# The FFN's output projection as a 2x2 block product of seven block products

## The chip, the core and the metric

The kernel runs on one core of a Trainium2 chip. The metric is device time in microseconds (us) of one execution. The engines are named as in the profile: PE is TensorE (matrix products, with PEld its weight loads), DVE is VectorE, ACT is ScalarE, POOL is GpSimd, SP is SyncE, which issues the DMAs.

## The reference

Two layers (DEPTH = 2) over a sequence of 512 rows of width 1024, in float32. Each layer is a token mixer (retention, chunk attention, differential attention, gates, a merge and one output projection), a layer norm, a SwiGLU FFN with 2816 hidden columns, and a second layer norm:

```python
x = _layer_norm(DEEPNORM_ALPHA * x + mix, ln1_g[l], ln1_b[l])
u = jnp.einsum('bsd,df->bsf', x, w_ffn_in[l])
u_gate, u_up = jnp.split(u, 2, axis=-1)
ffn = jnp.einsum('bsf,fd->bsd', jax.nn.silu(u_gate) * u_up, w_ffn_out[l])
x = _layer_norm(DEEPNORM_ALPHA * x + ffn, ln2_g[l], ln2_b[l])
```

The second einsum, 512 x 2816 by 2816 x 1024, is the output projection that is changed.

## The kernel before

Tiles have 128 rows. The sequence is NT = 4 row tiles `t`, the width KT = 8 tiles or two halves `hf` of 512 columns, the hidden width FT = 22 tiles. A float32 operand is carried as a pair `hi`, `lo` of float32r (class `Pair`; `split` makes it: ACT writes `hi`, DVE writes `lo`), and every product of two tiles is three matmuls (`mm3`): hi·hi, hi·lo, lo·hi. A weight (`Wt`) is loaded by SP into a staging tile `st` of up to 128 x 2048, cast by ACT to `wh` (L131) and subtracted by DVE to `wl` (L132), in two parts of 128 x 1024. There are NSTAGE staging tiles, AHEAD pairs of `wh` and `wl`, 8 PSUM banks and NSLOT = 60 slots of 128 x 512 in SBUF for everything else.

The program is a list of items, each with its weights and a function that issues its work. `run_items` takes the items in order and fetches weights of later items until AHEAD of them are ready. A list scheduler of the framework then sets the order of the instructions on each engine, from the order in which they were issued and from what they wait for; on each engine they run strictly in that order.

In the FFN a unit `u_ffn(i)` makes hidden tile i: 24 matmuls 512 wide for the gate, 24 for the other half, into two banks `pt`; ACT and DVE (`ffn_done`) turn them into `fth` and split it into the pair `hid[i]`. The first item, `u_ffn_first(2)`, does two units in halves of the sequence, since the transposes of the later half of the layer norm's rows come in its middle. Behind all 22 units comes the output projection, with hidden tiles as the stationary operand: `u_fout(hf, kb)` takes four hidden tiles and one weight 512 x 512 into four banks `pf`, one for each row tile; first all of half 0, then half 1, whose last four weights are one item, `u_fout_last`. That is 22 x 4 x 2 x 3 = 528 matmuls a layer. In this last item each row tile is finished on its own: residual and statistics (`fout_done`), and for the last layer `finish` (normalise and scale, store to the output), for the first layer `normalise` and, one row tile later, `transposes`, which put the rows into columns `xT` for the next layer (PE into banks `px`, ACT and DVE into pairs `xTh`, `xTl`). `natural` scales the rows and saves them.

The next layer begins with `u_first`: retention's first queries and keys (RQ, RK, 256 columns each) and the two halves of the values' weights; it starts on the first half of the sequence (256 columns) and calls `transposes(2)` and `transposes(3)` (`hooks`) behind that.

Of the kernel before, what the change touches and what calls it, by code (L numbers as in the profile page):

```python
# [2 lines left out]

# [8 lines left out]
F32 = mybir.dt.float32  # L12
# [28 lines left out]
PACKW = [512, 512, 256]  # L41

NSLOT = 60
AHEAD = 4
NSTAGE = 2
NLAST = 4


@with_exitstack
def trunk(ctx, tc, x_in, w_in, ret_norm_g, da_norm_g, lq1, lk1, lq2, lk2, w_a, w_b, w_c, b_merge, w_out,  # L50
# [23 lines left out]
    def bank(name="ps"):  # L74
        return psp.tile([P, 512], F32, tag="ps", name=name)
# [30 lines left out]
    class Wt:  # L106


        def __init__(self, pieces, nk, meanwhile=None):
# [19 lines left out]
            for a in range(0, nk, h):  # L129
# [3 lines left out]
                if meanwhile is not None and a == 0:  # L133
                    meanwhile()

    def proj_T(act, wt, c0, nk=KT, ps=None, half=None):
# [9 lines left out]
    def proj_T_half0(act, jobs, hook=None):  # L146

        for k in range(KT):
            a = act[k]
            if k == KT // 2 and hook is not None:  # L150
                hook()
# [102 lines left out]
    class Norm:  # L254
# [40 lines left out]
            if j == 1:  # L295
                self.to_T(hf)

        def to_T(self, hf):
            cols = slice(256 * hf, 256 * hf + 256)
            for k in range(KT):  # L300
# [32 lines left out]
    def run_items():  # L333
        ready, at = [], 0

        def fetch():
            nonlocal at
            specs, at = items[at][0], at + 1
            ready.append([])
            for sp in specs:  # L340
                first = at == 1 and not ready[-1]
                if first:
                    load_x(0, 2)
                ready[-1].append(Wt(*sp, meanwhile=first_x if first else None))
# [20 lines left out]
        load_x(2, NT)  # L365

    xTs = [[None] * KT for _ in range(DEPTH + 1)]
    hooks = {0: [lambda: start["n"].transposes(2), lambda: start["n"].transposes(3)]}

    def layer(l):  # L370
        lambda_init = 0.8 - 0.6 * math.exp(-0.3 * l)
# [78 lines left out]

        def u_first():

            def fn(wq, wk, *wv):
                ret_tables()
                pq, pk = [None] * 2, [None] * 2
                for j in range(2):
                    pq[j], pk[j] = bank("pt"), bank("pt")
                jobs = [(w, P * j, p[j]) for w, p in ((wq, pq), (wk, pk)) for j in range(2)]
                for js in ((jobs[:2], jobs[2:]) if l == 0 else (jobs,)):
                    proj_T_half0(xT, js)  # L460
                for hook in hooks[l]:
                    hook()
                for t in range(2):
                    rv_part(0, wv, t)
                for w, p, dst in ((wq, pq, rq), (wk, pk, rk)):
                    for j in range(2):
                        rqk_done(dst, j, proj_T(xT, w, P * j, ps=p[j], half=1))
                for t in range(2, NT):
                    rv_part(0, wv, t)
                vectors()  # L470
            return [([wcols(RQ, 256)], KT), ([wcols(RK, 256)], KT)] + rows_of(W, RV), fn

        def u_rg(hp):
            def fn(*wts):
# [304 lines left out]
            return mid, [s_d0(h, j)]  # L779

        for (specs, fn), *groups in [
            (u_first(),), (u_rg(0), [], [], [s_r1(0)], []),
            (u_rqk(rq, RQ, 1), [], [s_r2(0)]), (u_rqk(rk, RK, 1), [s_r1(1)], [s_r3(0)]),
            (u_rv(1), [s_r2(1)], [], [s_r3(1)], [s_r1(2)]), (u_rg(1), [], [s_r1(3)], [], []),
            (u_vhl(cv, CV, 64), [s_r2(2)], [s_r2(3)], [s_r3(2)], [s_r3(3)]), (u_cqk(0),),
            (u_gate(0, 0), *c(0)), (u_branch(0, 0), *c(1)), (u_cqk(1),),
# [63 lines left out]
        def ffn_spec(i):  # L850
            w = w_ffn_in[l]
            return ([w[:, P * i:P * i + P], w[:, FFN + P * i:FFN + P * i + P]], KT)

        def ffn_done(i, pg, pu):
# [7 lines left out]
        def u_ffn_first(n):  # L862
            def fn(*wts):
                pg, pu = [bank("pt") for _ in range(n)], [bank("pt") for _ in range(n)]
                proj_T_half0(x1T, [(wts[i], P * j, p[i]) for i in range(n) for j, p in enumerate((pg, pu))],
                             lambda: x1["n"].transposes(3))
                for i in range(n):
                    proj_T(x1T, wts[i], 0, ps=pg[i], half=1)
                    proj_T(x1T, wts[i], P, ps=pu[i], half=1)
                    ffn_done(i, pg[i], pu[i])  # L870
                for t in range(2, NT):
                    x1["n"].natural(t)
            return [ffn_spec(i) for i in range(n)], fn

        def u_ffn(i):
            def fn(wt):
# [2 lines left out]
                ffn_done(i, pg, pu)  # L879
            return [ffn_spec(i)], fn  # L880

        item(*u_ffn_first(2))
        for i in range(2, FT):
            item(*u_ffn(i))

        last = l == DEPTH - 1
        fo = {}
        x2 = {}

        def fout_done(hf, t):  # L890
            residual(x1["z"][t][hf], fo[hf][t])
            x2["n"].stats(t, hf)

        def u_fout(hf, kb):

            spec = rows_of(w_ffn_out[l], 512 * hf, 0, FT)[kb]

            def fn(wt):
                if kb == 0:
                    fo[hf] = [bank("pf") for _ in range(NT)]  # L900
                    if hf == 0:
                        load_res(saved[2 * l])
                        x2["n"] = Norm(x1["z"], v["g2"], v["b2"], bcast_rows(ln2_g[l:l + 1]),
                                       bcast_rows(ln2_b[l:l + 1]), xTs[l + 1], out if last else saved[2 * l + 1])
                for t in range(NT):
                    proj_N(hid, [wt], t, fo[hf][t], 4 * kb, kb == 0, 4 * kb + wt.nk == FT)
                    if 4 * kb + wt.nk == FT:
                        fout_done(hf, t)
            return [spec], fn

        def u_fout_last(kb):

            def fn(*wts):
                n = x2["n"]
                for t in range(NT):
                    proj_N(hid, wts, t, fo[1][t], 4 * kb, False, True)
                    if t in (1, 2) and not last:
                        n.transposes(t - 1)
                    fout_done(1, t)
                    if last:  # L920
                        n.finish(t)
                    else:
                        n.normalise(t)
                if not last:
                    n.natural(0)
                    n.natural(1)
            return rows_of(w_ffn_out[l], 512, 0, FT)[kb:], fn

        nb = -(-FT // 4)
        for kb in range(nb):  # L930
            item(*u_fout(0, kb))
        for kb in range(nb - NLAST):
            item(*u_fout(1, kb))
        item(*u_fout_last(nb - NLAST))

        def hook(t):
            def fn():
                x2["n"].transposes(t)
                if t == 3:
                    x2["n"].natural(2)  # L940
                    x2["n"].natural(3)
            return fn

        hooks[l + 1] = [hook(2), hook(3)]

    for l in range(DEPTH):
        layer(l)
# [47 lines left out]
```

## Time and profile before

| | |
|---|---|
| median of 3 runs | 1973.05 us (1972.7 to 1973.13) |
| the profiled execution | 1973.74 us, its span 1972.0 us |
| PE busy | 1953.1 us, 99% |
| DVE busy | 1045.0 us, 53% |
| ACT busy | 788.6 us, 40% |
| DMA | 203.21 MB, mean 103 GB/s |
| granted PE clock, mean | 0.998 |

The span is the stretch from the first to the last recorded event of the execution. Busy times of one engine are added up from single instructions; since matmuls are pipelined, the recorded duration of one is longer than the distance from its start to the next one's start. In the lines of a timeline stand the start, the duration, the engine, the line of the kernel, the operation, output<-inputs and, in brackets, the engine's idle time before and what ended it. In the lists of groups the numbers are the sum of busy time, the mean of one in ns and the idle time before.

### The profile page before, as it was taken

To read this page: it belongs to the slowest core of one execution; us is meant where nothing else is said; L and a number is where in the kernel's file an instruction comes from. 1 tells how busy PE (TensorE), PEld (TensorE's weight loads), DVE (VectorE), ACT (ScalarE), POOL (GpSimd) and SP (SyncE) were. 2 spreads that over 40 slices of the span, in tenths; PEclk is the share of its full clock that TensorE was granted. 3 is DMA by queue.
4 is the path that set the end of the run, shared out by engine and by line. 5 is a ranking of instruction groups with operands and counts; after the bars stand their busy time and mean duration, and the time that the engine had idled before them with its cause. 6 is when DMAs were issued, how large, how long until landed. Compare 5 with 4: busy or idle time off the path is not lost.

```text
span 1972.0 us, 23963 instructions
## 1 busy us (share of the span) xinstructions
PE 1953.1 (99%) x9506; PEld 1647.8 (84%) x9506; DVE 1045.0 (53%) x1918; ACT 788.6 (40%) x1431; POOL 48.2 (2%) x73
## 2 busy tenths in 40 slices
PE   8999999999999999999999999999999999999998
PEld 7888888888888888888898888888888898888886
DVE  4664556577557434333375545655774684343333
ACT  4443445466534322221154434555674343232220
POOL 0000000000000000000000000000000000000000
PEclk9999999999999999999999999999999999999999
DMA  5421332232145333242143223232221633332421
GB/s 187 135 89 56 118 102 82 74 97 75 64 150 163 106 96 100 92 159 97 62 163 118 75 86 102 76 90 86 86 86 48 209 109 111 102 95 98 160 75 43
DMA packets 222197, 203.21 MB, mean 103 GB/s; under 512 B 6926, under 2 KB 179076, under 8 KB 222084
## 3 DMA queue, kind: packets, MB, share of 16 engines
q1 hardware_dynamic: 222084, 201.67, 32.3%
q8 instruction: 75, 1.23, 0.3%
q14 instruction: 38, 0.31, 0.0%
HBM read 193.26 MB, written 8.39 MB: 102 GB/s over the span
## 4 chain that ended last, share of the span: by engine, by line
PE 98%; DVE 1%; DMA 0%; issue 0%; ACT 0%; SPq 0%; POOL 0%; DVEq 0%; ACTq 0%
PE pt L102 20%; PE pt L104 20%; PE pt L103 20%; PE pn L102 5%; PE pn L104 5%; PE pn L103 5%; PE pf L104 4%; PE pf L102 4%; PE pf L103 4%; PE ptr L238 1%; PE pco L625 1%; PE psc L209 1%; PE psc L208 1%; PE pdo L698 1%; PE po L104 1%; PE po L103 1%
## 5 line engine op out<-in xcount | busy, mean ns | idle before, releaser
L102 PE MATMUL pt<-xTh,wh 128*128 128x512 f32 (+1 forms) x1600 | 599.1, 375 | 4.6 <-ACT xTh L86 3.5
L103 PE MATMUL pt<-xTl,wh 128*128 128x512 f32 (+1 forms) x1600 | 596.0, 373 | 0.2 <-DVE xTl L92 0.2
L104 PE MATMUL pt<-xTh,wl 128*128 128x512 f32 (+1 forms) x1600 | 595.7, 373 | 0.0
L132 DVE TENSOR_TENSOR wl<-st,wh 128x1024 fp32r<-128x1024 f32 (+1 forms) x346 | 391.3, 1152 | 269.2 <-ACT wh L131 264.1
L131 ACT CAST wh<-st 128x1024 fp32r<-128x1024 f32 (+1 forms) x346 | 334.7, 997 | 483.5 <-PE pt L103 279.5
L102 PEld LDWEIGHTS pt<-xTh,wh 128*128 128x128 f32 x1600 | 302.2, 189 | 56.6 <-ACT xTh L86 3.9
L104 PEld LDWEIGHTS pt<-xTh,wl 128*128 128x128 f32 x1600 | 301.9, 189 | 53.1
L103 PEld LDWEIGHTS pt<-xTl,wh 128*128 128x128 f32 x1600 | 302.4, 189 | 51.8 <-DVE xTl L92 0.5
L102 PE MATMUL pn<-wh,xTh 128*128 128x512 f32 x384 | 151.0, 393 | 0.5 <-ACT lnt L307 0.5
L103 PE MATMUL pn<-wl,xTh 128*128 128x512 f32 x384 | 149.6, 390 | 0.0
L104 PE MATMUL pn<-wh,xTl 128*128 128x512 f32 x384 | 149.6, 390 | 0.0
L102 PE MATMUL pf<-wh,hidh 128*128 128x512 f32 x352 | 137.1, 390 | 0.0
L104 PE MATMUL pf<-wh,hidl 128*128 128x512 f32 x352 | 137.0, 389 | 0.0
L103 PE MATMUL pf<-wl,hidh 128*128 128x512 f32 x352 | 136.9, 389 | 0.0
L858 DVE TENSOR_TENSOR fth<-fth,pt 128x512 f32<-128x512 f32 x44 | 30.2, 687 | 170.3 <-PE pt L104 170.3
L104 PEld LDWEIGHTS pn<-wh,xTl 128*128 128x128 f32 x384 | 72.1, 188 | 15.2
L102 PEld LDWEIGHTS pn<-wh,xTh 128*128 128x128 f32 x384 | 72.1, 188 | 14.8 <-ACT lnt L307 0.7
L103 PEld LDWEIGHTS pn<-wl,xTh 128*128 128x128 f32 x384 | 72.2, 188 | 14.0
L857 DVE SCALAR_TENSOR_TENSOR fth<-fth,pt 128x512 f32<-128x512 f32 x44 | 30.2, 687 | 91.5 <-ACT fth L856 91.5
L103 PEld LDWEIGHTS pf<-wl,hidh 128*128 128x128 f32 x352 | 66.1, 188 | 13.7
L104 PEld LDWEIGHTS pf<-wh,hidl 128*128 128x128 f32 x352 | 66.1, 188 | 13.7
L102 PEld LDWEIGHTS pf<-wh,hidh 128*128 128x128 f32 x352 | 66.1, 188 | 13.6
(180 smaller groups left out, 2421.5 us busy)
## 6 DMA issues: line engine op xcount, KB each, us to landing
st<-in_w_in SPq DMA_DIRECT2D x55, 1024.0 KB
st<-in_w_ffn_in SPq DMA_DIRECT2D x88, 512.0 KB
st<-in_w_ffn_out SPq DMA_DIRECT2D x20, 1024.0 KB
st<-in_w_in SPq DMA_DIRECT2D x32, 512.0 KB
st<-in_w_branch_a SPq DMA_DIRECT2D x8, 1024.0 KB
st<-in_w_out SPq DMA_DIRECT2D x8, 1024.0 KB
saved<-z SPq DMA_DIRECT2D x24, 256.0 KB
z<-saved SPq DMA_DIRECT2D x24, 256.0 KB
```

The lines of the kernel that those rows point to most:

```text
L102: nc.tensor.matmul(ps, lh, rh, start=start, stop=False)
L103: nc.tensor.matmul(ps, lh, rl, start=False, stop=False)
L104: nc.tensor.matmul(ps, ll, rh, start=False, stop=stop)
L131: nc.scalar.copy(self.hi[:, a:b], st[:, a:b])
L132: nc.vector.tensor_sub(self.lo[:, a:b], st[:, a:b], f(self.hi[:, a:b]))
L208: nc.tensor.matmul(ps[:, :w], self.q[j][:, n], self.k[j][:, :w], start=True, stop=False)
L209: nc.tensor.matmul(ps[:, :w], self.q[j][:, n], self.kl[j][:, :w], start=False, stop=True)
L238: nc.tensor.transpose(ps[:, o + P * (nt - mt):o + P * (nt - mt) + P], E[pk][:, c + P * mt:c + P * mt + P], ident)
L625: nc.tensor.matmul(*x, start=mt == 0 and x is hi, stop=mt == NT - 1 and x is hi)
L698: nc.tensor.matmul(ps[:, 256 * j:256 * j + 256], pT[b].hi[:, o:o + P], vt[:, c:c + 256], start=mt == 0, stop=False)
L857: nc.vector.scalar_tensor_tensor(t, t, 1.0, pg, op0=ALU.add, op1=ALU.mult)
L858: nc.vector.tensor_mul(t, t, pu)
```

## The change

The output projection is done as a 2x2 block product with seven block products instead of eight. The hidden tiles are taken in three groups (`GROUPS`): first tile 0 with 2 x 4 tiles, 8 with 2 x 4, 16 with 2 x 3. Within a group the 512 rows are two halves, the group's hidden tiles two halves of kh tiles, the 1024 output columns two halves. `Quarters` takes two hidden tiles (i and i + kh) and makes the sums of row halves and tiles (`sa`, `sb`) and splits them: pairs `q11`, `q2`, `s12`, `s43`. `Halves` loads blocks of the weight and adds or subtracts them on DVE (`t1` to `t4`; `sa` is a staging tile of its own), `Staged` splits the result. Each product `m1, y, x, m2, v, g, h` runs for two row tiles j with kh x 3 matmuls, so that a layer has 7 x 2 x 22/2 x 3 = 462. Its bank is added to the residual `z` on DVE (`plus`), in `x` by way of `w` and `wy`, two copies that ACT made.

The items of a group's products are put between the units of the next group: a product, then one `u_ffn`. The last group has none behind it; its `g` and `h` are one item with two weights, which takes the place of `u_fout_last` (statistics, `finish` or `normalise`, `transposes`). AHEAD goes from 4 to 3, NSTAGE from 2 to 3. `u_first` now has three query and key weights (RQ, RK, RQ + 256), all three by halves of the sequence, with the transposes of the later rows in four parts (`transposes_of`) inside the third; the values' weights become an item of their own, and one item of the mixer's list goes.

```diff
-AHEAD = 4
-NSTAGE = 2
-NLAST = 4
+AHEAD = 3
+NSTAGE = 3
+GROUPS = [(0, 4), (8, 4), (16, 3)]
...
+    class Halves:
...
+        def t1(self):
+            self.add(self.a, self.load(0, 1))
+            return self.block(self.a)
...
+        def t4(self):
+            b, a = self.load(1, 0), self.__dict__.pop("a")
+            for s in self.parts():
+                nc.vector.scalar_tensor_tensor(b[:, s], a[:, s], -1.0, b[:, s], op0=ALU.mult, op1=ALU.subtract)
+            return self.block(b)
...
+    class Quarters:
...
+            nc.vector.tensor_sub(sa[:, a], t1[:, b], t2[:, b])
+            nc.vector.tensor_sub(sa[:, b], t1[:, a], sa[:, a])
+            nc.vector.tensor_sub(sb[:, a], t2[:, a], sa[:, b])
+            nc.vector.tensor_sub(sb[:, b], t1[:, b], t1[:, a])
+            q, p2, p12, p43 = g(F32R, "q11"), Pair("q2"), Pair("s12"), Pair("s43")
...
         def u_first():
-            def fn(wq, wk, *wv):
+            def fn(*wts):
...
+                banks.append([bank("pt") for _ in range(2)])
+                proj_T_half0(xT, [(wts[2], P * j, banks[2][j]) for j in range(2)],
+                             {2 * b: functools.partial(hooks[l], b) for b in range(4)})
...
         def ffn_done(i, pg, pu):
...
-            hid[i] = Pair("hid")
-            split(hid[i], t, scale=0.5)
+            hid[i] = t
+            r0, kh = next(x for x in GROUPS if x[0] <= i < x[0] + 2 * x[1])
+            if i >= r0 + kh:
+                hid[i - kh] = Quarters(hid[i - kh], hid[i], scale=0.5)
+                hid[i] = None
...
+        def plus(t, hf, ps, op, final=False):
...
+                nc.vector.tensor_tensor(z, z, ps, op=op)
+            if final:
+                x2["n"].stats(t, hf)
...
+            def x(wt):
+                for j in range(2):
+                    ps = run("x", j, wt)
+                    u = w.pop(j)
+                    nc.vector.tensor_sub(u, ps, u)
+                    plus(2 + j, 0, u, ALU.subtract)
+                    nc.vector.tensor_add(u, u, w.pop(("y", j)))
+                    plus(2 + j, 1, u, ALU.add)
+                    plus(j, 1, u, ALU.add)
...
+            def vv(wt):
+                for j in range(2):
+                    plus(j, 1, run("v", j, wt), ALU.add, end)
+                    if end:
+                        (x2["n"].finish if last else x2["n"].normalise)(j)
+
+            def g_(j, wt):
+                ps = run("g", j, wt)
+                plus(2 + j, 1, ps, ALU.add, end)
+                plus(2 + j, 0, ps, ALU.subtract)
+
+            def h_(j, wt):
+                ps = run("h", j, wt)
+                if end and not last:
+                    x2["n"].transposes(j)
+                plus(2 + j, 0, ps, ALU.subtract, end)
+                if end:
+                    (x2["n"].finish if last else x2["n"].normalise)(2 + j)
...
+            its = [([hv.b11], m1), ([hv.t1], y), ([hv.t2], x), ([hv.b21], m2), ([hv.b22], vv)]
+            return its + ([([hv.t3, hv.t4], gh)] if end else [([hv.t3], gg), ([hv.t4], hh)])
...
+        for gi in range(len(GROUPS)):
+            ids = tiles(gi + 1) if gi + 1 < len(GROUPS) else []
+            for it in fout_items(gi):
+                item(*it)
+                if ids:
+                    item(*u_ffn(ids.pop(0)))
```

How the instructions move, at three places. In the order's rows stand the line, the operation, output<-inputs, the shape and, for equal neighbours, their count.

DVE where layer 0 ends, before: `z` are the rows of the residual, `pf` a bank of the output projection, `bn`, `mv`, `rs` the norm's statistics, `bc` its scale, `xTl` the columns for the next layer.

```order
L285 TENSOR_SCALAR z<-z,mv,rs 128x512 x2
L805 SCALAR_TENSOR_TENSOR z<-z,pf 128x512
L314 TENSOR_TENSOR z<-z,bc 128x512
L92 TENSOR_TENSOR xTl<-lnt,xTh 128x256
L263 BN_STATS bn<-z 128x6
L315 TENSOR_TENSOR z<-z,bc 128x512
L92 TENSOR_TENSOR xTl<-lnt,xTh 128x256
```

And the same place in the changed kernel (`wl<-st,wh` of L134 are weights of the next layer's `u_first`):

```order
L997 TENSOR_TENSOR z<-z,pf 128x512
L419 TENSOR_TENSOR z<-z,bc 128x512
L997 TENSOR_TENSOR z<-z,pf 128x512 x2
L134 TENSOR_TENSOR wl<-st,wh 128x1024 x4
L357 BN_STATS bn<-z 128x6 x2
L374 BN_AGGR mv<-bn 128x2
L997 TENSOR_TENSOR z<-z,pf 128x512
L376 TENSOR_SCALAR rs<-mv 128x1
L94 TENSOR_TENSOR xTl<-lnt,xTh 128x256
L379 TENSOR_SCALAR z<-z,mv,rs 128x512 x2
```

The first `xTl` now stands behind additions to `z` of all products and behind four splits of the next unit's weights.

PE at the same place, before: the transposes of a row tile (`px`), followed by more products of the output projection.

```order
L104 MATMUL pf<-wh,hidl 128x512
L294 MATMUL px<-ident,z 128x128 x8
L102 MATMUL pf<-wh,hidh 128x512
L103 MATMUL pf<-wl,hidh 128x512
L104 MATMUL pf<-wh,hidl 128x512
```

And in the changed kernel, around the second set of transposes:

```order
L104 MATMUL pf<-wh,q2h 128x512
L105 MATMUL pf<-wl,q2h 128x512
L106 MATMUL pf<-wh,q2l 128x512
L388 MATMUL px<-ident,z 128x128 x8
L104 MATMUL pt<-xTh,wh 128x256 x3
L105 MATMUL pt<-xTl,wh 128x256
```

Directly behind the second transposes now stands the next layer's first unit; the first transposes have two products of nine matmuls behind them.

DVE at the end of the program, before:

```order
L275 SCALAR_TENSOR_TENSOR z<-z,rs,bc 128x512 x2
L805 SCALAR_TENSOR_TENSOR z<-z,pf 128x512
L263 BN_STATS bn<-z 128x6
L268 BN_AGGR mv<-bn 128x2
L270 TENSOR_SCALAR rs<-mv 128x1
L273 SCALAR_TENSOR_TENSOR z<-z,mv,bc 128x512 x2
L275 SCALAR_TENSOR_TENSOR z<-z,rs,bc 128x512 x2
```

And changed:

```order
L193 SCALAR_TENSOR_TENSOR st<-sa,st 128x512 x3
L206 TENSOR_TENSOR wl<-st,wh 128x512 x3
L997 TENSOR_TENSOR z<-z,pf 128x512 x2
L357 BN_STATS bn<-z 128x6 x2
L997 TENSOR_TENSOR z<-z,pf 128x512 x2
L357 BN_STATS bn<-z 128x6 x2
L362 BN_AGGR mv<-bn 128x2
L997 TENSOR_TENSOR z<-z,pf 128x512
L364 TENSOR_SCALAR rs<-mv 128x1
L367 SCALAR_TENSOR_TENSOR z<-z,mv,bc 128x512 x2
L369 SCALAR_TENSOR_TENSOR z<-z,rs,bc 128x512 x2
```

Before, one row tile's half was left for the end; now weight sums and splits, the additions of the last four products and all four row tiles' finishing follow one another in DVE's queue.

More of the change, by code (lines that the diff above doesn't have):

```diff
@@ L1 @@
+import functools
 import math
@@ new lines, in trunk, with __init__ @@
+    class Quarters:
+        def __init__(self, t1, t2, scale=None):
+            a, b = slice(0, 256), slice(256, 512)
+            sa, sb = g(name="sa"), g(name="sb")
+            nc.vector.tensor_sub(sa[:, a], t1[:, b], t2[:, b])
[3 more added lines that the diff above has]
+            q, p2, p12, p43 = g(F32R, "q11"), Pair("q2"), Pair("s12"), Pair("s43")
+            part_hi(q[:, a], t1[:, a], scale)
+            part_lo(q[:, b], t1[:, a], q[:, a], scale)
+            split(p2, t2, scale=scale)
+            split(p12, sa, scale=scale)
+            split(p43, sb, scale=scale)
+            self.use = {"m1": (q[:, a], q[:, b])}
+            for names, pr in ((("m2", "h"), p2), (("y", "x"), p12), (("v", "g"), p43)):
+                for name, sl in zip(names, (a, b)):
+                    self.use[name] = (pr.hi[:, sl], pr.lo[:, sl])
@@ L144, in proj_T, with proj_T_half0 @@
         return ps
-    def proj_T_half0(act, jobs, hook=None):
+    def proj_T_half0(act, jobs, hooks):
         for k in range(KT):
             a = act[k]
-            if k == KT // 2 and hook is not None:
-                hook()
+            if k in hooks:
+                hooks[k]()
             for wt, c0, ps in jobs:
@@ L296, in transposes, with transposes_of, to_T @@
                 self.to_T(hf)
-        def to_T(self, hf):
+        def transposes_of(self, hf, b):
+            ps = bank("px")
+            self.banks[hf] = {b: ps}
+            for k in (2 * b, 2 * b + 1):
+                for j in range(2):
+                    o = 256 * (k % 2) + P * j
+                    nc.tensor.transpose(ps[:, o:o + P],
+                                        self.z[2 * hf + j][k // 4][:, P * (k % 4):P * (k % 4) + P], ident)
+            self.to_T(hf, (2 * b, 2 * b + 1))
+        def to_T(self, hf, ks=range(KT)):
             cols = slice(256 * hf, 256 * hf + 256)
-            for k in range(KT):
+            for k in ks:
                 if self.xT[k] is None:
@@ L367, in trunk @@
     xTs = [[None] * KT for _ in range(DEPTH + 1)]
-    hooks = {0: [lambda: start["n"].transposes(2), lambda: start["n"].transposes(3)]}
+    hooks = {0: lambda b: start["n"].transposes_of(1, b)}
     def layer(l):
@@ L911, in u_fout_last @@
[L911 to L944, printed above, removed]
+        def plus(t, hf, ps, op, final=False):
+            z = x1["z"][t][hf]
+            if (t, hf) in x2["fresh"]:
+                x2["fresh"].remove((t, hf))
+                nc.vector.scalar_tensor_tensor(z, z, ALPHA, ps, op0=ALU.mult, op1=op)
+            else:
+                nc.vector.tensor_tensor(z, z, ps, op=op)
+            if final:
+                x2["n"].stats(t, hf)
@@ new lines, in fout_items, with run, m1, y @@
+        def fout_items(gi):
+            r0, kh = GROUPS[gi]
+            end = gi == len(GROUPS) - 1
+            hv = Halves(w_ffn_out[l], r0, kh)
+            w = {}
+            def run(name, j, wt):
+                ps = bank("pf")
+                for k in range(kh):
+                    hi, lo = hid[r0 + k].use[name]
+                    sl = slice(P * j, P * j + P)
+                    mm3(ps, hi[:, sl], lo[:, sl], wt.hi[:, k], wt.lo[:, k], k == 0, k == kh - 1)
+                return ps
+            def m1(wt):
+                if gi == 0:
+                    load_res(saved[2 * l])
+                    x2["fresh"] = {(t, hf) for t in range(NT) for hf in range(2)}
+                if end:
+                    x2["n"] = Norm(x1["z"], v["g2"], v["b2"], bcast_rows(ln2_g[l:l + 1]),
+                                   bcast_rows(ln2_b[l:l + 1]), xTs[l + 1], out if last else saved[2 * l + 1])
+                for j in range(2):
+                    ps = run("m1", j, wt)
+                    w[j] = g(name="w")
+                    nc.scalar.copy(w[j], ps)
+                    plus(j, 0, ps, ALU.add)
+            def y(wt):
+                for j in range(2):
+                    ps = run("y", j, wt)
+                    w["y", j] = g(name="wy")
+                    nc.scalar.copy(w["y", j], ps)
+            def x(wt):
+                for j in range(2):
+                    ps = run("x", j, wt)
[5 more added lines that the diff above has]
+                    plus(j, 1, u, ALU.add)
+            def m2(wt):
+                for j in range(2):
+                    plus(j, 0, run("m2", j, wt), ALU.add, end)
+            def vv(wt):
+                for j in range(2):
+                    plus(j, 1, run("v", j, wt), ALU.add, end)
[10 more added lines that the diff above has]
+                plus(2 + j, 0, ps, ALU.subtract, end)
+                if end:
+                    (x2["n"].finish if last else x2["n"].normalise)(2 + j)
+            def gg(wt):
+                for j in range(2):
+                    g_(j, wt)
+            def hh(wt):
+                for j in range(2):
+                    h_(j, wt)
+            def gh(wg, wh):
+                for j in range(2):
+                    g_(j, wg)
+                    h_(j, wh)
+                if not last:
+                    x2["n"].natural(0)
+                    x2["n"].natural(1)
+            its = [([hv.b11], m1), ([hv.t1], y), ([hv.t2], x), ([hv.b21], m2), ([hv.b22], vv)]
+            return its + ([([hv.t3, hv.t4], gh)] if end else [([hv.t3], gg), ([hv.t4], hh)])
@@ new lines, in tiles @@
+        def tiles(gi):
+            r0, kh = GROUPS[gi]
+            return [r0 + i + kh * j for i in range(kh) for j in range(2)]
+        ids = tiles(0)
+        item(*u_ffn_first(ids[:2]))
+        for i in ids[2:]:
+            item(*u_ffn(i))
+        for gi in range(len(GROUPS)):
[4 more added lines that the diff above has]
+                    item(*u_ffn(ids.pop(0)))
+            for i in ids:
+                item(*u_ffn(i))
```

108 lines of the change are left out of this document (64 added, 44 removed).

## The prediction

> **What bounds the kernel now.** I read the page first: busy shares, chain of waits, costliest groups.
>
> ```profile
> span 1972.0 us, 23963 instructions
> PE 1953.1 (99%) x9506; PEld 1647.8 (84%) x9506; DVE 1045.0 (53%) x1918; ACT 788.6 (40%) x1431; POOL 48.2 (2%) x73
> PE 98%; DVE 1%; DMA 0%; issue 0%; ACT 0%; SPq 0%; POOL 0%; DVEq 0%; ACTq 0%
> L102 PE MATMUL pf<-wh,hidh 128*128 128x512 f32 x352 | 137.1, 390 | 0.0
> L104 PE MATMUL pf<-wh,hidl 128*128 128x512 f32 x352 | 137.0, 389 | 0.0
> L103 PE MATMUL pf<-wl,hidh 128*128 128x512 f32 x352 | 136.9, 389 | 0.0
> ```
>
> TensorE (PE) is the bound: 99% busy, 98% of the chain, and its 3 × 352 = 1056 output-projection matmuls (`pf`) wait for nothing. Outside its busy time only 1972.0 − 1953.1 = 18.9 us are left in the span. The mean of 390 ns is no price, because matmuls overlap. The windows by stage (columns: window; length, busy time and count of the engine; clock; DMA share; GB/s) give the pitch, first for PE, then for VectorE (DVE):
>
> ```profile
> 700.00:900.00 200.00, 200.00 (x884) 1.00 0.37 113
> 1000.00:1010.00 10.00, 9.54 (x57) 1.00 0.74 271
> ```
>
> ```profile
> 700.00:900.00 200.00, 73.05 (x84) 1.00 0.37 113
> 900.00:960.00 60.00, 18.03 (x21) 1.00 0.28 97
> 1960.00:1972.00 12.00, 4.39 (x8) 0.90 0.20 75
> ```
>
> A 512-wide matmul comes every 200/884 = 0.226 us (0.2266 between neighbours in the timeline). VectorE is idle two thirds of the FFN; that is the cover the change wants to use. The third view is the timeline at the end, where the tail after the last matmul stands, with VectorE's prices:
>
> ```profile
> 1964.01 0.39 PE L104 MATMUL pf<-wh,hidl 128*128 128x512 f32 x1
> 1964.43 0.69 DVE L805 SCALAR_TENSOR_TENSOR z<-z,pf 128x512 f32<-128x512 f32 x1 [5.03 <-PE pf L104]
> 1965.15 0.69 DVE L263 BATCH_NORM_STATS2 bn<-z 128x6 f32<-128x512 f32 x1
> 1965.88 0.21 DVE L268 BATCH_NORM_AGGREGATE mv<-bn 128x2 f32<-128x12 f32 x1
> 1966.12 0.15 DVE L270 TENSOR_SCALAR rs<-mv 128x1 f32<-128x1 f32 x1
> 1966.19 1.40 DVE L273 SCALAR_TENSOR_TENSOR z<-z,mv,bc 128x512 f32<-128x512 f32 x2
> 1967.52 1.41 DVE L275 SCALAR_TENSOR_TENSOR z<-z,rs,bc 128x512 f32<-128x512 f32 x2
> ```
>
> The last matmul ends at 1964.40, VectorE at 1968.93, the span at 1972.0: a tail of 7.6 us, of which 3.07 are the output's DMA. Here a finishing operation costs 1.33/2 = 0.66 us by starts, an operation that needs the one before it 0.72, the aggregate 0.24, the small one 0.07. VectorE waited 5.03 us for PE before this.
>
> **The change part by part.**
>
> *Matmuls saved.* The order shows 924 `pf` matmuls for 1056. 132 × 0.2266 = −29.9 us.
>
> *Half-width columns.* The first unit's third weight is done in halves: 96 matmuls of 512 become 192 of 256.
>
> ```profile
> 997.05 0.28 PE L103 MATMUL pt<-xTl,wh 128*128 128x256 f32 x1
> 997.17 0.28 PE L104 MATMUL pt<-xTh,wl 128*128 128x256 f32 x1
> ```
>
> Starts are 0.12 apart: 96 × (2 × 0.120 − 0.2266) = +1.3.
>
> *VectorE in the mixed phase.* Between products stands a 48-matmul unit, so a product and its unit last 72 × 0.2266 = 16.3 us. VectorE's rows for the price:
>
> ```profile
> 969.46 0.69 DVE L805 SCALAR_TENSOR_TENSOR z<-z,pf 128x512 f32<-128x512 f32 x1 [6.02 <-PE pf L104]
> 970.06 0.69 DVE L314 TENSOR_TENSOR z<-z,bc 128x512 f32<-128x512 f32 x1
> 970.66 0.69 DVE L263 BATCH_NORM_STATS2 bn<-z 128x6 f32<-128x512 f32 x1
> 971.27 0.68 DVE L315 TENSOR_TENSOR z<-z,bc 128x512 f32<-128x512 f32 x1
> 985.22 1.00 DVE L285 TENSOR_SCALAR z<-z,mv,rs 128x512 f32<-128x512 f32 x2 [0.47 <-POOL rs L283]
> 986.14 1.22 DVE L132 TENSOR_TENSOR wl<-st,wh 128x1024 fp32r<-128x1024 f32 x1
> 987.28 0.42 DVE L92 TENSOR_TENSOR xTl<-lnt,xTh 128x256 fp32r<-128x256 f32 x1
> 987.61 2.36 DVE L132 TENSOR_TENSOR wl<-st,wh 128x1024 fp32r<-128x1024 f32 x2
> ```
>
> By starts: 0.60 for 128x512 on two tensors, 1.14 for 128x1024, 0.33 for 128x256, 0.92/2 = 0.46 for a normalise. A unit costs 73.05/(884/48) = 4.0 now. Added per unit are half a pair's quarter sums and splits (5 × 0.33 + 3 × 0.60, halved: 1.7), less the old 0.60 split; per product the weight's split 2.28, on four of seven a weight sum 2.28, and two additions to `z` 1.2 (ten operations in product `x`). That makes about 11 of 16.3 us, about 16 for `x`, and a weight is split at least 10 us before its product by my walk through the order. ScalarE (40% busy) gets two copies of 128x512 per product and the quarters' casts, and the DMA, at a share of 0.28 to 0.37 in these windows, loads seven quarter blocks of weights for four. PE does not wait for any of them: 0. If that cover went, the price is the second rival's.
>
> *The last group, layer 1.* It has no units between: 7 products × 18 × 0.2266 = 28.6 us of PE, against 44 us of VectorE's queue. Put t = 0 at the end of the group before. Product `x`'s first bank is done at 10.25; its evacuation cannot come earlier, and behind it the order has, in one queue: 20 operations on weights and `w`/`z` (12.0), 10 additions to `z` and 8 statistics (10.8), 16 finishing operations (10.6), four aggregates and small ones (1.3), and some dependent pairs at 0.72 instead of 0.60: 35.2 us. So VectorE ends at 45.5 at the earliest; in my walk, where weight sums ahead of `x` delay the start to about 12, at 47.2. With the DMA's 3.07 the span ends 20.0 to 21.7 after PE's 28.6, where now it is 7.6: +12.4 to +14.1, and 14.5 if the evacuation slips further. I take the walk: +14.1.
>
> *The last group, layer 0.* The same queue stands before the next layer's first unit. From `x`'s evacuation to the first `xTl`, the order has 37 operations of 0.60 (22.2), six weight splits of 1.14 for that unit (6.8), four normalises (1.8), small ones and `xTl` (1.3) and about 1 us of dependent pairs: 33 us. So the unit starts at 44 (earliest 43.3) to 46, where PE alone would be there at 30.5. Part of it PE waits earlier, at `transposes(0)`, which has two products behind it in PE's queue. With the unit's own half columns (96 × 0.12 = 11.5) PE stands at 55.5 to 57.5 instead of 42; now the boundary costs 10 − 9.54 = 0.46. +13.0 to +14.8, taken +14.3. What is late next is nothing on PE's side; the work itself is not shortened.
>
> *The clock after these idles.* PE would stand idle 5 to 7 us at a stretch. The one such stretch in this trace is at the start:
>
> ```profile
> 11.51 0.58 PE L102 MATMUL pt<-xTh,wh 128*128 128x256 f32 x1 [3.21 <-ACT xTh L86]
> 13.11 0.41 PE L103 MATMUL pt<-xTl,wh 128*128 128x256 f32 x1
> 13.32 0.41 PE L104 MATMUL pt<-xTh,wl 128*128 128x256 f32 x1
> 16.95 0.38 PE L102 MATMUL pt<-xTh,wh 128*128 128x256 f32 x1
> 17.16 0.28 PE L103 MATMUL pt<-xTl,wh 128*128 128x256 f32 x1
> ```
>
> After it matmuls come 0.21 apart until 16.95, 5.4 us after the first, against 0.12 later. That is 25 matmuls × 0.09 = 2.3 lost, if an idle in mid-kernel does the same; the 0.46 idle at 1000 left the clock at 1.00. Bounds 0 to 2.4, taken half: +1.2, since a start-up is not an idle after work. [...]
>
> *Look-ahead 4 to 3.* The FFN's first unit needs two weights. In the order two weight splits now come ahead of `normalise(2)`, after which PE has `transposes(2)`.
>
> ```profile
> 627.71 0.39 PE L102 MATMUL pt<-xTh,wh 128*128 128x256 f32 x1 [0.56 <-DVE z L805]
> ```
>
> One split more of 1.14 on that path makes a wait of 0.56 into 1.7: +1.2 in each layer, +2.4 (0 to 3). In the mixer, units with two weights keep at least 2 us of lead by my walk, and the first unit's three weights fill all three buffers; a product `m1` may wait a few tenths for a group's last quarters. Nothing shows these: between −2 (no more can be gained: of the 18.9 us outside PE's busy time, 7.6 are the tail and most of the rest lies before 17 us) and +3. Taken +1.6, nearer the cost, because the buffers get fewer.
>
> *Sum:* −29.9 + 1.3 + 14.1 + 14.3 + 1.2 + 2.4 + 1.6 = +5.0. On the profiled execution (1973.74, its span 1972.0 and 1.74 around it) that is 1978.7; it lies 0.69 above the median of the runs, 1973.05, on which I predict **1978.0**. The ends: −29.9 + 1.3 + 12.4 + 13.0 + 0 + 0 − 2 = −5.2 and −29.9 + 1.3 + 14.5 + 14.8 + 2.4 + 3 + 3 = +9.1, so 1968 to 1982.
>
> **The rivals.**
>
> *A, faster: VectorE is quicker than its rows.* The new operations mostly have operands like the normalise's, of 0.46. If all two-tensor operations ran at 0.46, the tail's queue would shrink by 38 × 0.14 + 16 × 0.20 = 8.5 (+5.6 left), the boundary's by 37 × 0.14 + 6 × 0.22 = 6.5 (+7.8 left), idles would be too short for the clock: −29.9 + 1.3 + 5.6 + 7.8 + 2.4 + 1.6 = −11.2, 1962. It decides once about 8 us of the two queues together vanish, also by the sums lying further ahead of PE than I walked. Against it: `wl<-st,wh` has two operands like the new sums and costs 1.14 for 1024. [...] Chance 0.12.
>
> *B, much slower: each product waits.* A summed weight passes load, sum, cast, split, the sums and splits in VectorE's queue behind additions to `z` that wait for PE, with three buffers. If that lead of 10 us is not there, a wait of 0.5 us at each of 42 products is 21 us less what the last groups wait anyway (14 products, 7): +14 more, 1992. It decides where VectorE's share of a product and unit passes 16.3 us; `x` with about 16 is at the edge, the next product gives back 5. Chance 0.15.
>
> That the matmuls do not go is excluded by the order's 924.
>
> **How the numbers follow.** My forecast, the two last groups bound by VectorE with the rest hidden, has 0.73, with its own range 1968 to 1982. A change under 0.2% (3.9 us, about what a measurement of this kernel can tell) is 1969.1 to 1977.0; of the forecast some 0.30 lies in there, 0.02 below and 0.41 above. With A below and B above: faster 0.14, same 0.30, slower 0.56. The range is the forecast's own and the nearer part of B: 1968 to 1989.
>
> **What would show it.** Right: PE's matmul count falls by 132 `pf` and the sum of its busy time by about 29; VectorE full for about 35 us before the end, a tail near 21 after the last matmul; a PE idle of some 14 us in all around the layer boundary, ended by VectorE's `z` and `xTl`; and no idle at `pf` in the mixed phase. Wrong: a tail under 14 us or a boundary idle under 8 (A), or idle time ahead of `pf` matmuls over a few us in all, ended by `wl` or `z` (B).

## The result: no change that can be measured

Over 12 runs each the changed kernel takes 1973.53 us (1972.12 to 1975.93) against 1972.88 (1972.14 to 1973.39): a ratio of 1.0004 with a 95% interval of 0.9996 to 1.0013. The profiled execution took 1973.63 us, its span is 1971.8, against 1972.0 before.

The page of the changed kernel, the lines on busy times, and the windows of the FFN's middle, first for PE, then for DVE:

```profile
span 1971.8 us, 24443 instructions
PE 1930.1 (98%) x9470; PEld 1632.8 (83%) x9470; DVE 1248.1 (63%) x2272; ACT 856.2 (43%) x1549; POOL 47.1 (2%) x73
```

```profile
700.00:900.00 200.00, 200.00 (x882) 1.00 0.42 128
```

```profile
700.00:900.00 200.00, 133.11 (x176) 1.00 0.42 128
```

PE is busy 23 us less (1953.1 before) while the span stayed. In the middle nothing is lost: PE is full, with 882 matmuls in 200 us against 884, although VectorE now works 133.1 of the 200 us instead of 73.1. So the time must be given back elsewhere, and PE's waits say where (columns: what waited, for what; us in all, times, longest):

```profile
PE px L388 <- DVE z L379: 8.6, 3, 5.2
PE pt L104 <- ACT xTh L88: 4.9, 2, 2.8
...
PE pt L104 <- DVE rs L376: 2.1, 1, 2.1
```

There is no wait at `pf` at all. The waits for `z` are the first norm's transposes (1.71 us in each layer) and one of 5.2 us at the layer boundary; of the two for `xTh` one is at the start (2.76 us) and one at the boundary. The timeline of PE there, with the first matmul of the last group (t = 0), the waits, and the end of the next unit's first half:

```profile
945.85 0.39 PE L104 MATMUL pf<-wh,q 128*128 128x512 f32 x1
...
970.53 0.40 PE L106 MATMUL pf<-wh,q2l 128*128 128x512 f32 x1
976.14 1.97 PE L388 MATMUL px<-ident,z 128*128 128x128 f32 x8 [5.21 <-DVE z L379]
977.76 0.78 PE L104 MATMUL pf<-wh,s43h 128*128 128x512 f32 x1
978.34 0.63 PE L105 MATMUL pf<-wl,s43h 128*128 128x512 f32 x1
978.76 0.63 PE L106 MATMUL pf<-wh,s43l 128*128 128x512 f32 x1
...
987.08 0.50 PE L104 MATMUL pt<-xTh,wh 128*128 128x256 f32 x2 [2.11 <-ACT xTh L88]
989.66 0.58 PE L104 MATMUL pt<-xTh,wh 128*128 128x256 f32 x1 [2.09 <-DVE rs L376]
...
1003.75 0.60 PE L399 MATMUL px<-ident,z 128*128 128x128 f32 x4
```

PE idles 5.21 + 2.11 + 2.09 = 9.41 us, and the products that follow the first idle start 0.43 apart instead of 0.23. The windows (PE's busy time and count, then the granted clock) show the same:

```profile
970.00:980.00 10.00, 4.79 (x17) 0.76 0.72 237
980.00:990.00 10.00, 5.81 (x25) 0.84 0.54 199
990.00:1000.00 10.00, 10.00 (x63) 0.72 0.55 185
```

VectorE's timeline carries it. At the layer boundary: `x`'s first evacuation, the four splits of the next unit's weights, the first column `xTl`:

```profile
957.32 0.69 DVE L1039 TENSOR_TENSOR w<-pf,w 128x512 f32<-128x512 f32 x1
...
983.12 4.63 DVE L134 TENSOR_TENSOR wl<-st,wh 128x1024 fp32r<-128x1024 f32 x4 [0.44 <-ACT wh L133]
...
989.59 0.42 DVE L94 TENSOR_TENSOR xTl<-lnt,xTh 128x256 fp32r<-128x256 f32 x1
```

And at the program's end, PE's last matmul among VectorE's rows:

```profile
1934.22 0.69 DVE L1039 TENSOR_TENSOR w<-pf,w 128x512 f32<-128x512 f32 x1
...
1951.10 0.39 PE L106 MATMUL pf<-wh,q2l 128*128 128x512 f32 x1
...
1967.21 1.41 DVE L369 SCALAR_TENSOR_TENSOR z<-z,rs,bc 128x512 f32<-128x512 f32 x2
```

VectorE runs from `x`'s evacuation to 1968.62 in one piece, 34.4 us, and the span ends 1971.8 − 1951.49 = 20.3 us after the last matmul, where it was 7.6.

### The profile page after: what moved, and what is told of

It is laid out like the page before. It is cut to its first block, busy times and chain, and to the rows that moved or that the text cites. A ratio compares the mean times of both kernels' runs of the same rounds, so it can differ in the third digit from the quotient of the medians.

```text
span 1971.8 us, 24443 instructions
## 1 busy us (share of the span) xinstructions
PE 1930.1 (98%) x9470; PEld 1632.8 (83%) x9470; DVE 1248.1 (63%) x2272; ACT 856.2 (43%) x1549; POOL 47.1 (2%) x73
## 3 DMA queue, kind: packets, MB, share of 16 engines
q1 hardware_dynamic: 230820, 218.98, 35.2%
## 5 line engine op out<-in xcount | busy, mean ns | idle before, releaser
L104 PE MATMUL pt<-xTh,wh 128*128 128x512 f32 (+1 forms) x1632 | 606.2, 372 | 7.0 <-ACT xTh L88 4.9
L105 PE MATMUL pt<-xTl,wh 128*128 128x512 f32 (+1 forms) x1632 | 603.2, 370 | 0.2 <-DVE xTl L94 0.2
L106 PE MATMUL pt<-xTh,wl 128*128 128x512 f32 (+1 forms) x1632 | 603.0, 370 | 0.0
L134 DVE TENSOR_TENSOR wl<-st,wh 128x1024 fp32r<-128x1024 f32 (+1 forms) x298 | 339.4, 1154 | 161.7 <-ACT wh L133 159.2
L104 PEld LDWEIGHTS pt<-xTh,wh 128*128 128x128 f32 x1632 | 309.5, 190 | 57.6 <-ACT xTh L88 5.5
L106 PEld LDWEIGHTS pt<-xTh,wl 128*128 128x128 f32 x1632 | 309.5, 190 | 51.6
L105 PEld LDWEIGHTS pt<-xTl,wh 128*128 128x128 f32 x1632 | 310.1, 190 | 50.7 <-DVE xTl L94 0.5
L104 PEld LDWEIGHTS pn<-wh,xTh 128*128 128x128 f32 x384 | 72.1, 188 | 14.2
L960 ACT ACTIVATE fth<-pt 128x512 f32<-128x512 f32 x44 | 26.3, 598 | 121.4 <-PE pt L106 121.4
L267 ACT COPY sw<-pt 32x512 f32<-32x512 f32 (+1 forms) x96 | 55.7, 580 | 31.0 <-PE pt L106 29.8
L205 ACT CAST wh<-sa 128x1024 fp32r<-128x1024 f32 (+1 forms) x42 | 34.4, 865 | 75.8 <-PE pt L105 55.8
L319 ACT ACTIVATE cE<-cE,mx 128x512 f32<-128x512 f32 (+1 forms) x64 | 35.3, 553 | 60.9 <-DVE mx L318 60.9
```

The costliest lines, as they stand in the source:

```text
L104: nc.tensor.matmul(ps, lh, rh, start=start, stop=False)
L105: nc.tensor.matmul(ps, lh, rl, start=False, stop=False)
L106: nc.tensor.matmul(ps, ll, rh, start=False, stop=stop)
L134: nc.vector.tensor_sub(self.lo[:, a:b], st[:, a:b], f(self.hi[:, a:b]))
L205: nc.scalar.copy(self.hi[:, s], st[:, s])
L267: nc.scalar.copy(sw[half * b:half * b + half], ps[half * o:half * o + half])
```

## The experiments

Theory V: the saved 30 us go back in the two last groups, where no unit of the FFN covers VectorE's queue. Rival P: they go back a little at each product. Further rivals are H (transposes block PE's queue), C (the clock) and the look-ahead. "Plain" below means eight block products, accumulated in PSUM. The kernel before took 1972.88, 1973.21, 1973.46 and 1973.24 us in the four groups of runs from which the medians here come, so differences of some tenths between groups mean nothing.

**The last six hidden tiles plain, in both layers.**

```diff
+            if l in PLAIN and i >= 16:
+                hid[i] = Pair("hid")
+                split(hid[i], t, scale=0.5)
+                return
...
-            for it in fout_items(gi):
+            for it in ([plain(0), plain(1)] if l in PLAIN and gi == 2 else fout_items(gi)):
...
+                for t in range(NT):
+                    ps = bank("pf")
+                    proj_N(hid, wts, t, ps, 16)
+                    if hf and t in (1, 2) and not last:
+                        n.transposes(t - 1)
+                    plus(t, hf, ps, ALU.add, True)
+                    if hf:
+                        (n.finish if last else n.normalise)(t)
```

`plain(hf)` has two weights and is the item for one half of the output columns. The next layer's first unit then does its first two weights one after the other instead of together.

> In both layers the last six hidden tiles are projected in the plain way (eight block products in PSUM, no sums), the first sixteen as in the changed kernel. This costs 18 matmuls a layer more: 36 x 0.2266 = +8.2 us. Theory V (VectorE's queue in the last groups gives the saved time back: 12.7 us in the tail and about 15 at the layer boundary): both come back nearly whole, the tail to about 8 us after the last matmul, the boundary to 0 to 6 us of waiting, since the next unit's weight splits still stand among its columns: 1973.5 + 8.2 - 12.5 - 10 to -15 = 1954 to 1960. Rival P (the time is given back between the products and units, a little at each of 42 products): nothing comes back from the last groups, a seventh less of the small waits: 1976 to 1982.

Measured: 1956.45 us (1955.77 to 1960.15), 0.992 of the kernel before, interval 0.9906 to 0.9933. V holds, P falls. The edit takes VectorE's sums, ScalarE's copies and the added loads out together, so it shows the place; that VectorE's queue is the cause is read from the changed kernel's waits. PE's waits of this run:

```profile
PE px L389 <- DMA xn<-in_x: 4.5, 2, 3.7
PE px L389 <- DVE z L380: 3.9, 2, 2.2
PE pt L105 <- ACT xTh L89: 2.7, 1, 2.7
...
PE pt L106 <- DVE xTl L95: 0.5, 2, 0.3
```

At the boundary nothing is left but 0.34 us for a column; the other waits are the program's start, the two FFN starts (2.24 and 1.71) and 0.8 us in the mixers. The last matmul and the end of VectorE's work:

```profile
1945.92 0.39 PE L107 MATMUL pf<-wh,hidl 128*128 128x512 f32 x1
...
1950.42 1.41 DVE L370 SCALAR_TENSOR_TENSOR z<-z,rs,bc 128x512 f32<-128x512 f32 x2
```

With a span of 1954.9 the tail is 8.6 us. So 36 matmuls more made the kernel 17 us faster than the changed one.

**The same in one layer only.** `PLAIN` is (0,) and (1,).

> The plain way for the last six hidden tiles in layer 0 only (18 matmuls more, +4.1 us). Theory V: the layer boundary's cost goes, the tail stays at 20 us: 1973.5 + 4.1 - 10 to -15 = 1963 to 1968. Rival P: 1975 to 1978.

> The plain way for the last six hidden tiles in layer 1 only (18 matmuls more, +4.1 us). Theory V: the tail goes from 20 back to about 8 us, the boundary stays: 1973.5 + 4.1 - 12.5 = 1964 to 1966, and with the run before it the two gains add up to that of the kernel with both. Rival P: 1975 to 1978.

Measured: 1964.96 us (ratio 0.9958, 0.9942 to 0.9973) and 1965.33 (0.9961, 0.9947 to 0.9974). Against 1973.53 that is 8.6 and 8.2 us, together 16.8, where both at once gave 17.1: the two places add up. With the 4.1 us for 18 matmuls given back in each, the boundary had cost 12.7 us and the tail 12.3, and the trace of the second, plain in layer 1 only, still has the boundary's waits whole:

```profile
PE px L389 <- DVE z L380: 8.6, 3, 5.2
...
PE pt L105 <- DVE z L1002: 2.2, 1, 2.2
```

Each median is of four runs that spread over 3 us, so the shares are rough. By the traces the boundary costs about 2 us more: from the last group's first matmul to the end of the next unit's first half it is 57.9 us in the changed kernel and 995.32 − 948.26 = 47.1 in the first of the two, with 4.1 of it for the matmuls added. That profiled execution also reached the last group 2.4 us later.

**Transposes behind the last product.**

```diff
-                if end and not last:
-                    x2["n"].transposes(j)
+                if end and not last and j:
+                    x2["n"].transposes(0)
+                    x2["n"].transposes(1)
```

> In layer 0's last group both sets of transposes come behind the last product, so that PE does not wait for a normalise with two products behind it. Theory V (VectorE's queue sets when the next unit's columns are there, PE's idle is only its shadow): the idle of 5.2 us moves behind the two products, the end of the boundary stays where it is but for the 0.44 us that VectorE waited for a weight's cast: 1972.5 to 1973.5. Rival H (the transposes block PE's queue, and the two products behind them hold up all that follows): 4 to 5 us faster, 1968.5 to 1969.5.

Measured: 1972.82 us (1971.27 to 1973.65; ratio 0.9997, 0.9989 to 1.0006), 0.7 under the changed kernel's median. H falls as priced. From the last group's first matmul to the end of the next unit's first half:

```profile
948.03 0.39 PE L104 MATMUL pf<-wh,q 128*128 128x512 f32 x1
...
1003.83 0.60 PE L399 MATMUL px<-ident,z 128*128 128x128 f32 x4
```

This took 55.8 us against 1003.75 − 945.85 = 57.9: 2.1 shorter, more than the 0.44 that V gave and half of what H asked. VectorE's first column shows where it comes from:

```profile
990.79 0.42 DVE L94 TENSOR_TENSOR xTl<-lnt,xTh 128x256 fp32r<-128x256 f32 x1
```

It comes 42.8 us after the group's first matmul, where it was 43.7 in the changed kernel; the other 1.1 us lie behind it, in the unit's half, 13.0 us for 14.2. A shorter stretch at half clock accounts for them: it ends at about 994.2 (the mean clock is 0.50 from 992 to 994, 0.94 from 994 to 996), 3.4 us behind the column, where the changed kernel's ends 6.0 behind it. The run as a whole shows less of it: the last group's first matmul, ahead of which the two programs should not differ, comes at 948.03 and 945.85. That gap is there at the first FFN's start already (629.01 and 626.83) and comes from the program's start, which varies: PE waits 2.63 us for a part of the input here and 1.77 there, and the clock averages 0.92 from 30 to 40 us here and 1.00 there.

**The clock kept up.** Idle matmuls that do nothing for the output fill PE's two waits:

```diff
+                        for _ in range(40):
+                            nc.tensor.matmul(n.banks[0][0][:, :256], a[:, :P], b, start=True, stop=True)
                     x2["n"].transposes(j)
...
+                    for _ in range(50):
+                        nc.tensor.matmul(banks[0][0][:, :256], a[:, :P], b, start=True, stop=True)
```

> The changed kernel with 40 idle matmuls (128x256, their result is overwritten) ahead of the first transposes of layer 0's last group and 50 ahead of the next layer's first unit, where PE now waits about 5 us each time; they do no work for the output. In the changed kernel's trace the granted clock is at a half for 6.8 us twice in this place. Theory C (the clock costs time of its own: the next unit's first half ran at matmuls 0.21 apart for some 5 us and so fell behind VectorE's columns): the clock stays at 1.00 and the half ends with VectorE's last columns, about 3 us sooner: 1970 to 1971.5. Rival V alone (PE only follows VectorE there, a slow clock hides in its waits): 1973 to 1974, the same.

Measured: 1971.03 us (1969.24 to 1973.09; ratio 0.9988, 0.998 to 0.9997), 2.5 below the changed kernel. The windows:

```profile
970.00:980.00 10.00, 9.17 (x64) 1.00 0.85 292
980.00:990.00 10.00, 10.00 (x73) 1.00 0.71 236
990.00:1000.00 10.00, 9.79 (x79) 1.00 0.30 112
```

The clock stays at 1.00. From the first matmul of the group (947.92) to the end of the half (1002.48) it is 54.6 us, 3.3 shorter. Not all of it need be the clock's, since VectorE's first column is earlier too:

```profile
982.66 4.63 DVE L134 TENSOR_TENSOR wl<-st,wh 128x1024 fp32r<-128x1024 f32 x4
...
990.31 0.42 DVE L94 TENSOR_TENSOR xTl<-lnt,xTh 128x256 fp32r<-128x256 f32 x1
```

It comes 42.4 us after the group's first matmul, not 43.7: the wait of 0.44 ahead of the four splits is gone, and VectorE's order differs (a scaling `z<-z,bc` of 0.60 that stood ahead of the column now stands behind it). From this column to the end of the half it is 12.2 us for 14.2. So C holds in the run's time, and of the 3.3 us some 2 are the clock's; for the other 1.3 clock and order were not told apart.

**Weight sums three times.** In the groups of four, that is the first two. The edit reaches `add`, which makes `t1`, `t2` and `t3`; `t4` has an operation of its own and stays:

```diff
+                if self.kh == 4:
+                    nc.vector.tensor_add(t[:, s], t[:, s], u[:, s])
+                    nc.vector.tensor_sub(t[:, s], t[:, s], u[:, s])
                 nc.vector.tensor_add(t[:, s], t[:, s], u[:, s])
```

> In the first two groups of each layer every weight sum is done three times (added, taken off, added): 2 x 2.28 = 4.6 us more of VectorE at four of seven products, 16 sums of this kind in the program, 73 us of VectorE's time. Theory V (outside the last groups VectorE has 5 us to spare in each product and unit of 16.3, with weights 10 us ahead): the same to 3 us slower, 1973.5 to 1976.5. Rival P (each product waits for its summed weight): a good part of the 73 us is seen, 1990 and more.

Measured: 1973.74 us (1973.06 to 1976.25; ratio 1.0003, 0.9993 to 1.0012): nothing of the added work is seen. It is less than expected, three sums of four, 12 in the program: VectorE's busy time goes from 1248.1 to 1302.2 us, 54 more and not 73. The time is 0.2 us from the changed kernel's, so P falls. VectorE's window, and the only wait at a product, which is in layer 0's last group (at 971.41), where no sum was repeated:

```profile
700.00:900.00 200.00, 155.45 (x198) 1.00 0.42 126
```

```profile
PE pf L105 <- DVE wl L209: 0.2, 1, 0.2
```

So 54 us of added VectorE work were free between units, where VectorE then works 155.5 us of 200. In the last groups I estimate that it would cost its full length, since VectorE's queue at the end has no gap in 34.4 us; no run adds any there.

**The look-ahead alone.** The kernel before with `AHEAD = 3`, `NSTAGE = 3`, `NLAST = 3`:

> The kernel before with the look-ahead of the changed one alone: three weights ahead instead of four and three staging tiles instead of two (the last item has three weights instead of four, to fit). By the wait of 1.71 us instead of 0.56 at the start of each FFN, seen in the changed kernel: +2.3, 1975.0 to 1976.0. Rival (that wait comes with the other changes, or three staging tiles give it back): no change, 1972.5 to 1973.5.

Measured: 1974.2 us (1973.31 to 1974.76; ratio 1.0004, 0.9996 to 1.0013). The runs of the kernel before beside it have 1973.46, so +0.7, and the interval holds no change at all: neither number was right. PE's waits of this run, and then those of before:

```profile
PE px L294 <- DVE z L285: 3.4, 2, 1.7
```

```profile
PE psc L208 <- DVE ocl L94: 1.1, 2, 0.6
PE pt L102 <- DVE z L805: 1.1, 2, 0.6
PE pn L102 <- ACT lnt L307: 0.5, 1, 0.5
PE pt L102 <- DVE dPl L92: 0.3, 2, 0.2
```

The wait at the FFN's start is there, 3.4 us for 1.1, but the mixer's waits of 1.1 and 0.3 are gone with it. A wait of 0.43 for a weight's split at 993.07 is new.

**Four weights ahead again.** The plain kernel with `AHEAD = 4`, `NSTAGE = 2`, `NSLOT = 57`:

> The kernel with the plain last six tiles in both layers, with four weights ahead and two staging tiles as in the kernel before, and 57 slots instead of 60 to make room. If the look-ahead costs what the waits at the FFN's starts show, 2.3 us less: 1953.5 to 1955. If two staging tiles are too few for the sums, which need two loads each, PE waits at products: 1956 to 1962.

Measured: 1972.29 us (0.9994, 0.9985 to 1.0003), 16 us slower than the plain kernel. Neither reason given covers that, so the slots and the staging tiles were changed one at a time:

> The kernel with the plain last six tiles in both layers, with 57 slots instead of 60 and nothing else changed. The kernel with four weights ahead lost 16 us against the plain one, among it four waits of 2.3 us for the chunk attention's keys, each followed by 3.4 us at half clock. If the three slots are the cause: those waits are here too, 1966 to 1973. If not: 1955.5 to 1958.

> The same kernel with two staging tiles instead of three and 60 slots, three weights ahead. If two staging tiles are the cause of those waits or hold up the summed weights: 1960 or more. If not: 1955.5 to 1958.

Measured: 1977.95 us (1.0021, 1.0012 to 1.0031) with 57 slots, 1955.97 (0.9911, 0.9894 to 0.9927) with two staging tiles. The slots are the cause, and at a price above the 1966 to 1973 expected, 21.5 us. The waits with 57, and the granted clock around one of them:

```profile
PE psc L303 <- ACT ks L89: 9.2, 4, 2.3
```

```profile
291.00:298.00 7.00, 4.70 (x18) 0.76 0.23 87
```

These four waits and the 3.4 us at half clock behind each (a mean of 0.76 over 7 us: 2 × 0.24 × 7), of which I count half as lost, make 9.2 + 6.8 = 16 us as an estimate; the rest was not followed up. The kernel with four weights ahead, two staging tiles and the same 57 slots is 5.7 us faster than this one (1972.29), so the look-ahead itself costs nothing there.

The last kernel, with two staging tiles, and the plain one with three (1956.45) are the fastest here; their difference is within what the runs vary.

## Why the prediction was right, and where not

The forecast was +5.0 on the profiled execution, within 1968 to 1989; the profiled span changed by −0.2, the median by +0.65, 4.5 us under the 1978.0 named. A slower kernel had the larger chance, 0.56 against 0.30 for no change. The mechanism is the one forecast, and the one-layer experiments show it: what PE saved went back at two places, and nowhere between units. That the two sides cancel to under 1 us is chance: the forecast had 28.6 us saved and 33.6 given back.

- *Matmuls saved, −29.9.* The pitch held (882 for 884 in 200 us), so the price by pitch and not by the mean of 390 ns was right. That much is in the traces; no run took the matmuls away alone. PE's busy time fell by 23.0, not by the 29 named as a sign: matmuls at half clock at the boundary are recorded longer (0.63 us for 0.39 at 512 wide, 0.41 for 0.28 at 256), by the 6 us estimated below.
- *Half-width columns, +1.3.* The starts are 0.12 apart in the changed kernel too (64 steps from 995.95 to 1003.63), so the price held in the traces; no run took it alone.
- *VectorE in the mixed phase, 0.* Right: 133.1/200 is 67%, as 11 of 16.3 us, and even 78% costs nothing (sums three times).
- *The tail, +14.1.* Measured +12.7. The queue was 34.4 us long, forecast 35.2; the evacuation came at 11.3 after the group's start by the last matmul less 28.6, where I had 12.
- *The boundary, +14.3, and the clock, +1.2.* The half ended at t = 57.9, forecast 55.5 to 57.5 ahead of the clock's term. VectorE's first `xTl` was there at t = 43.7, where the unit was to start at 44 to 46, so its queue was a little shorter. The unit's half then took 14.2 us instead of 11.5, since PE ran at half clock to about 995.6: the clock cost 2.0 (by the run that keeps it up) to 2.7 on this path, about twice the 1.2. The parts that PE shows were mis-sized: idle 9.41 − 0.46 = 8.95, not 14.3, because the products at half clock filled time that I had counted as idle. The mean clock over 970 to 1000 is 0.77, 13.7 us at half, of which PE worked about 12 (the ends of two waits, 0.9 us each, fall into them), so it lost about 6. Idle and loss together, 15, are near to the 15.5 forecast, which is in part luck: the shorter queue and the dearer clock cancel.
- *Look-ahead at the FFN's start, +2.4.* Measured 2 × (1.71 − 0.56) = +2.3.
- *All else, +1.6.* This is the term that failed in sign. The mixer's waits of 1.1 and 0.3 us went away instead of new ones coming, and at the start the idle is the same within 0.2. The kernel before with three weights ahead loses the same mixer waits. About −1.3 for +1.6, 2.9 us of the 5.2 by which the span missed the sum; the tail is 1.4 of it, boundary and clock between 0.1 (by the half's end) and 0.6 (by idle and loss).

Rival A (a quicker VectorE) had no part: the four splits of the next unit took 4.63 us, 1.14 each by starts as before. That the idles left in it would be too short for the clock no run shows: it stayed at 1.00 behind waits of 1.71 and 2.24 us, and fell to half behind waits of 2.28 to 2.31 (last section). Rival B fell with the traces, which have no wait at `pf`, and with the sums three times.

## What to carry to other kernels

Here work moved from the bound engine to an idle one was free only where it had other work of the bound engine beside it: 54 us more of it between units changed the time by 0.2 us, while the two last groups cost 12.7 and 12.3. So price each stage by its own queue, the last one and every boundary above all. The trade paid in two groups of three, and leaving the third out turned no change into 0.8% faster. Before buying look-ahead with buffers of another pool, see who waits for those: three slots of sixty cost the plain kernel 21 us.

## What the runs showed that was not expected

The clock fell also after shorter waits than the 3.21 us at the program's start from which I had priced it. With 57 slots PE idled only 2.31 us at a stretch, and the matmuls behind it ran slower:

```profile
293.69 1.44 PE L303 MATMUL psc<-ks,qs 128*128 128x512 f32 x4 [2.31 <-ACT ks L89]
294.92 0.74 PE L105 MATMUL pt<-xTh,wh 128*128 128x512 f32 x1
```

In the window from 291 to 298 of that run, shown above, the granted clock averages 0.76, which is 3.4 us of the seven at a half. The waits at the FFN's starts left no such mark, neither 1.71 us (the changed kernel's clock is 1.00 from 626.83 to 640) nor the 2.24 in layer 0 of the plain kernel, here with the window behind it; that kernel's mean clock is 0.999:

```profile
627.18 1.11 PE L389 MATMUL px<-ident,z 128*128 128x128 f32 x8 [2.24 <-DVE z L380]
```

```profile
627.00:640.00 13.00, 12.82 (x108) 1.00 0.75 222
```

With 57 slots a stretch at half clock came behind waits of 2.28 to 2.31 us, all four of them; in layer 1, behind the 2.30 at 1272.08, the 512-wide matmuls come 0.43 apart from 1274.40 to 1276.53, then 0.23. Behind 2.24 it did not come, so the length alone, by so small a difference, may not decide. What does was not tried.
